# The start of a hybrid decoder step: normalization in written order, query weights loaded by contraction tiles, and products without a reader between them

## The chip, the cores and the metric

The program runs on one core of a Trainium2 chip. The time of a run is the device time of that core in microseconds (us). Three runs of the kernel before gave 1644.03, 1644.74 and 1642.79 us; their median, 1644.03 us, is the number that the predicted time is compared with. The engines are named as in the profile: PE (matrix products), ACT, DVE and POOL (elementwise work, casts, copies), SP (it issues transfers). POOL and ACT issue transfers as well. Every engine takes its instructions in the order in which they stand in its own queue, and waits at the head of that queue until what the instruction needs is there.

## The reference

One layer of a decoder is applied to 512 prompt rows with 16 learned rows ahead of them, and to 8 x 4 sample rows with caches: T = 560 rows of width 2048 in all. What matters here is its beginning:

```python
def rmsnorm(x, g):
    xf = x.astype(jnp.float32)
    y = xf * lax.rsqrt(jnp.mean(xf * xf, axis=-1, keepdims=True) + RMS_EPS)
    return (y * g.astype(jnp.float32)).astype(x.dtype)
...
    h = rmsnorm(x, g_pre)
    q, k, v, ga, cb, cc, ch, gc, ma, mc = jnp.split(h @ w_in, split_offsets(), axis=-1)
...
    a = attend(q, k, v, b_sb).reshape(bsz, t, D_ATTN) * jax.nn.silu(ga)
    u = cc * ch
    u_ext = jnp.concatenate([conv_hist.astype(u.dtype), u], axis=1)
    c = cb * causal_conv(u_ext, w_conv, b_conv) * jax.nn.silu(gc)
    merged = (jax.nn.sigmoid(ma + b_gate[:D_MODEL]) * (a @ w_pa)
              + jax.nn.sigmoid(mc + b_gate[D_MODEL:]) * (c @ w_pc))
    y = x + rmsnorm(merged @ w_out, g_post)
```

Everything is float32. There are 8 heads of width 128, so a head's queries are 128 columns of w_in. The sample rows read keys and values from pages that page_table names.

## The kernel before, in words

A float32 product is made of three products of reduced-precision parts: every operand is split into a high part (a cast, on ACT) and a low part (operand minus high part, on DVE), and high x high, high x low and low x high are summed. A product of 2048 input columns is a sum over 16 contraction tiles k of 128 columns; one group of 48 matmuls (16 k, three parts) gives 128 output columns for some 280 rows.

**The start stage** (all code up to `stx.close()`) normalizes the input and computes the queries of the first four heads (`FIRST = 4`), of which the later stages make use. Its parts:

- The rows come in five tiles (`XT`): x0 and x1 hold prompt rows 0 to 255, x2 and x3 the next 248, x4 the last 8 prompt rows, the sample rows and half of the learned rows (48 rows); x2 holds the other learned rows. They are loaded by SP into three buffers `xt`.
- `norm_stats(i)` loads a tile, squares and sums each row on ACT (`sq`), and takes Ln and Exp for a first reciprocal root (`rtmp`); `newton` sharpens it in five small operations on DVE (`rs`).
- The gain `g_pre` is spread over the partitions by 32 small matmuls on PE into four PSUM tiles `g_ps`, copied to `g_bc` by `g_copy(c)`. Ten 128x512 products of a constant, with no reader (`warm_up`, tile `tp`), stand ahead of them.
- `norm_half(c, x)` multiplies half a tile by `rs` and `g_bc` on DVE (`hn`), transposes it on PE in two groups of four (into the PSUM tiles z, of which there are three, and tp), casts each group to `h_hi` on ACT and subtracts on DVE into `h_lo`. One half covers eight contraction tiles k.
- `q_load(h)` loads the weights of head h in two units of eight contraction tiles (`raw`, 512 KB), and casts them (`whi`, ACT). The low parts (`wlo`) come later, by `low()`, on DVE.
- `START` cuts the rows into the 256 of x0 and x1 and the other 296. For the first 256, the products with the high weights of all four heads run before the tiles x4, x2, x3 are normalized, and the products with the low weights (`parts (2,)`) after it, together with the 296 rows.

What sets the order: PE's, ACT's, DVE's, POOL's and SP's instructions are ordered at build time by a scheduler with a model of time. `tc.keep_in_program_order` (`pin`) holds an instruction to the written order; `tc.high_priority` moves one ahead. Before the change, the multiplications, low parts and newton steps on DVE are pinned, the transposes and the casts of h on ACT have high priority, and the query products, the casts of weights and the loads are free.

**Buffers**: `wraw` has five tiles `raw`, `whl` three each of `hi` and `lo` (they serve the whole kernel), and `sp` is a pool of the start stage alone; what other pools place over its memory has to wait for `stx.close()`, that is for its last reader.

**After the start stage**: the tables `bsb` (the heads' bias), `pt_i` (the page table, from which POOL reads 32 register values by `value_load` before it can issue page loads), `bg_n`, `wc_n` and `st_n` are loaded by POOL. Then `head_now(0)` computes k, v and another query projection on PE (line 252 before), while `q_proj` stores the queries of the first heads through `qn` into `q_scr` by POOL; the decode steps read them back as `qb` (POOL), multiply them with pages `kpage` on DVE (`pr`) and sum on ACT or DVE. `natural` transposes k and v on PE into tp, copies them to `nat` and `ks`, and POOL stores them (`out<-nat`); `nat` is one buffer, so that v's copy waits until k's store has landed.

Of the kernel before, what the change touches and what calls it, by code (L numbers as in the profile page):

```python
# [60 lines left out]
def hybrid_step_kernel(  # L61
# [58 lines left out]
    def load_x(xt, i):  # L120
        r = 0
        for n, src, r0 in XT[i][0]:
            nc.sync.dma_start(xt[r:r + n, :], {"p": xp, "m": meta_tokens, "s": xs}[src][r0:r0 + n, :])
            r += n

    def rstd_of(eng, out, ss, tmp, n, w=1, later=False):

        v, r, t = (tmp[:n, i * w:(i + 1) * w] for i in range(3))
        act.activation(r, ss, AF.Ln, bias=eps_c[:n], scale=1.0 / D)
        act.activation(r, r, AF.Exp, scale=-0.5)  # L130
# [39 lines left out]
    for c, mk in enumerate((mm_ps, mm_ps, mm_ps, z_ps)):  # L170
# [11 lines left out]

    start_ps = cycle((z_ps, z_ps, z_ps, t_ps))

    def norm_stats(i):

        n = sum(r[0] for r in XT[i][0])
        xt = sp.tile([P, D], F32, name="xt", bufs=3)[:n]
        load_x(xt, i)
        ss = sp.tile([P, 1], F32, name="ss", bufs=5)[:n]  # L190
# [3 lines left out]
        with tc.high_priority():  # L194
            act.activation(sq, xt, AF.Square, accum_out=ss)
            newton = rstd_of(dve, rs, ss, tmp, n, later=True)
        return (i, n, xt, rs), newton

    def norm_half(c, x):
# [7 lines left out]
        low = []  # L207
        for kq in range(2):
            pt = next(start_ps)()
            pv = pt[:, :4 * n].rearrange("p (k t) -> p k t", t=n)  # L210
            with tc.high_priority(2000):
                for k in range(4):
                    pe.transpose(out=pv[:, k, :], in_=hn[:, (4 * kq + k) * P:(4 * kq + k + 1) * P],
                                 identity=ident[:n, :n])
            k0 = 8 * c + 4 * kq
            for r0, r1, t0 in XT[i][1]:
                dst = (slice(None), slice(k0, k0 + 4), slice(t0, t0 + r1 - r0))
                with tc.high_priority(2000):
                    act.copy(h_hi[dst], pv[:, :, r0:r1])
                low.append((h_lo[dst], pv[:, :, r0:r1], h_hi.bitcast(F32)[dst]))  # L220

        def lows():
            for x in low:
                pin(dve.tensor_sub(*x))
# [1097 lines left out]
```

## Time and profile before

| | |
|---|---|
| median of three runs | 1644.03 us |
| the profiled execution | 1641.85 us |
| its span, first to last instruction | 1640.3 us |
| PE busy in the span | 1594.9 us (97%) |
| DVE, ACT, POOL busy | 1251.8, 970.1, 232.4 us |
| mean granted PE clock | 0.99 |
| first product after the start stage (line 252) | at 86.40 us |

The profiled execution stands 1.55 us above its own span and 2.18 us under the median of the runs. A row of the timeline gives the start in us from the first instruction, the length in us, the engine, the line, the operation, the tiles written and read, their shapes and a count where equal instructions follow each other; a bracket gives the idle time before it and what ended it. Rows of the windows give, for a stretch of time, the busy time of each engine with its count of instructions, then the granted PE clock, the share of the DMA engines and GB/s. Matmuls overlap each other, so the pace of a row of matmuls is read from start to start, not from their lengths.

### The profile page before, as it was taken

What the parts mean: (1) busy time and instruction counts of PE and PEld (TensorE: products, weight loads), DVE (VectorE), ACT (ScalarE), POOL (GpSimd) and SP (SyncE); (2) the same over time, 40 slices, a digit from 0 to 9 for tenths busy, and PEclk for the clock granted to TensorE, in tenths of its full rate; (3) what the DMA queues carried; (4) which work ended last, traced back from release to release, by engine and by line L of the source; (5) the groups of instructions that cost most, each with busy time, mean ns of one, the idle gap of its engine ahead of it and who ended that gap; (6) DMA issues with size and microseconds to landing.
All of it is one profiled execution on the core that took longest, in us unless ns stands there. A gap on an engine that the chain in (4) does not pass through costs nothing.

```text
span 1640.3 us, 31584 instructions
## 1 busy us (share of the span) xinstructions
PE 1594.9 (97%) x12176; PEld 1531.3 (93%) x12176; DVE 1251.8 (76%) x1707; ACT 970.1 (59%) x2529; POOL 232.4 (14%) x414
## 2 busy tenths in 40 slices
PE   7999999999999999999999999999999999999996
PEld 6999999999999999999999999989867699999995
DVE  4537887797988988888988888876555567877774
ACT  5237887745765655655677667685544543455552
POOL 0033233322101010101011010013122110000000
PEclk7999999999999999999999999999999999999998
DMA  9255454445544444443455454446887555433336
GB/s 228 70 179 152 155 160 139 146 128 170 157 147 136 136 135 122 127 142 111 137 164 161 149 174 148 135 125 204 283 261 222 172 152 179 154 106 94 104 87 216
DMA packets 306492, 252.72 MB, mean 154 GB/s; under 512 B 11457, under 2 KB 276741, under 8 KB 305237
## 3 DMA queue, kind: packets, MB, share of 16 engines
q1 hardware_dynamic: 277605, 159.73, 34.1%
q0 software_dynamic: 28016, 88.80, 16.5%
q8 instruction: 95, 1.56, 0.4%
q10 hardware_dynamic: 720, 2.17, 0.4%
q14 instruction: 56, 0.46, 0.1%
HBM read 217.95 MB, written 32.71 MB: 153 GB/s over the span
## 4 chain that ended last, share of the span: by engine, by line
PE 75%; ACT 6%; DMA 5%; DVE 5%; issue 3%; POOL 0%; DVEq 0%; SPq 0%; POOLq 0%; ACTq 0%
PE mm L887 24%; PE mm L252 24%; PE o L887 19%; ACT junk L695 3%; PE tp L784 2%; ACT whi L236 2%; DMA raw<-in_w_in 2%; PE z L614 1%; PE o L624 1%; DVE pr L689 1%; DVE wlo L237 1%; DMA gt<-gate_scr 1%; PE z L545 1%; PE z L887 1%; DMA kpage<-in_cache_k 1%
## 5 line engine op out<-in xcount | busy, mean ns | idle before, releaser
L236 ACT CAST whi<-raw 128x1024 fp32r<-128x1024 f32 x251 | 263.1, 1050 | 258.5 <-PE o L887 79.3
L237 DVE TENSOR_TENSOR wlo<-raw,whi 128x1024 fp32r<-128x1024 f32 x251 | 306.4, 1221 | 58.0 <-ACT whi L236 46.1
L887 PE MATMUL mm<-h_hi,whi 128*128 128x272 f32 (+1 forms) x1152 | 333.5, 290 | 2.8 <-ACT whi L236 2.8
L887 PE MATMUL mm<-h_lo,whi 128*128 128x272 f32 (+1 forms) x1152 | 332.1, 288 | 0.0
L887 PE MATMUL mm<-h_hi,wlo 128*128 128x272 f32 (+1 forms) x1152 | 331.3, 290 | 0.0
L887 PE MATMUL o<-t_hi,whi 128*128 128x272 f32 (+1 forms) x864 | 252.2, 292 | 8.5 <-ACT o L901 5.9
L887 PE MATMUL o<-t_hi,wlo 128*128 128x272 f32 (+1 forms) x864 | 249.9, 289 | 1.4 <-DVE wlo L237 1.4
L887 PE MATMUL o<-t_lo,whi 128*128 128x272 f32 (+1 forms) x864 | 249.6, 289 | 0.0
L237 DVE TENSOR_TENSOR wlo<-s,whi 128x1024 fp32r<-128x1024 f32 x126 | 154.2, 1224 | 101.5 <-ACT whi L236 101.2
L887 PEld LDWEIGHTS mm<-h_hi,whi 128*128 128x128 f32 x1152 | 217.3, 189 | 5.5 <-ACT whi L236 3.7
L887 PEld LDWEIGHTS mm<-h_hi,wlo 128*128 128x128 f32 x1152 | 216.3, 189 | 0.6 <-DVE dr L412 0.4
L887 PEld LDWEIGHTS mm<-h_lo,whi 128*128 128x128 f32 x1152 | 216.8, 188 | 0.1
L695 ACT ACTIVATE junk<-pr 128x128 f32<-128x128 f32 x592 | 182.7, 309 | 28.3 <-DVE pr L689 16.1
L236 ACT CAST whi<-s 128x1024 fp32r<-128x1024 f32 x126 | 131.6, 1044 | 97.5 <-PE o L887 31.0
L252 PE MATMUL mm<-h_hi,whi 128*128 128x280 f32 (+1 forms) x640 | 187.1, 293 | 0.0
L252 PE MATMUL mm<-h_hi,wlo 128*128 128x280 f32 (+1 forms) x640 | 187.0, 293 | 0.0
L252 PE MATMUL mm<-h_lo,whi 128*128 128x280 f32 (+1 forms) x640 | 186.7, 292 | 0.0
L887 PEld LDWEIGHTS o<-t_hi,whi 128*128 128x128 f32 x864 | 162.7, 188 | 15.1 <-ACT o L901 7.0
L887 PEld LDWEIGHTS o<-t_hi,wlo 128*128 128x128 f32 x864 | 162.9, 189 | 2.3 <-DVE wlo L237 2.2
L887 PEld LDWEIGHTS o<-t_lo,whi 128*128 128x128 f32 x864 | 163.4, 189 | 0.0
L689 DVE TENSOR_TENSOR pr<-kpage,qb 128x1024 f32<-128x1024 f32 x128 | 152.3, 1218 | 8.4 <-DMA kpage<-in_cache_k 4.0
L252 PEld LDWEIGHTS mm<-h_hi,whi 128*128 128x128 f32 x640 | 120.5, 188 | 0.7
(389 smaller groups left out, 3398.2 us busy)
## 6 DMA issues: line engine op xcount, KB each, us to landing
raw<-in_w_in SPq DMA_DIRECT2D x192, 512.0 KB, 4.3
kpage<-in_cache_k POOLq DMA_DIRECT2D x64, 256.0 KB, 3.4
qb<-q_scr POOLq DMA_DIRECT2D x32, 512.0 KB, 5.3
vpage<-in_cache_v POOLq DMA_DIRECT2D x64, 256.0 KB, 5.7
raw<-in_w_out SPq DMA_DIRECT2D x32, 512.0 KB, 4.0
gate_scr<-g POOLq DMA_DIRECT2D x32, 272.0 KB, 3.2
gt<-gate_scr POOLq DMA_DIRECT2D x16, 544.0 KB, 4.2
raw<-in_w_pc SPq DMA_DIRECT2D x16, 512.0 KB, 5.8
```

Source lines behind the costliest of these rows:

```text
L236: act.copy(hi, x)
L237: dve.tensor_sub(lo, x, hi.bitcast(F32))
L252: pe.matmul(o, lhsT=w, rhs=r[:, t0:t1], start=(k == 0 and n == 0), stop=(k == nk - 1 and n == 2))
L545: pe.matmul(zt[:m, c0:c0 + n], lhsT=l[:, s0:s0 + m], rhs=r[:, ts:ts + n], start=(c0 == 0 and i == 0), stop=(i == 2), skip_group_check=True)
L614: pe.matmul(o, lhsT=l, rhs=x, start=False, stop=(i == len(ops) - 1), skip_group_check=True)
L624: pe.matmul(ot[:, ts - NMETA:ts - NMETA + n], lhsT=l[:m, st, :], rhs=x[:m, c0:c0 + n], start=False, stop=(g == GROUPS[-1] and i == 2), ski ...
L689: dve.tensor_mul(pr, kt.unsqueeze(1).broadcast_to([P, 2, 512]), qt))
L695: act.activation(junk, pr[:, t, h * P:(h + 1) * P], AF.Copy, accum_out=z_all[:, pg, b, 4 * hf + h, 2 * i + t:2 * i + t + 1])
L784: pe.matmul(po[32 * j:32 * (j + 1), :], lhsT=lhs, rhs=rhs, start=(pg == 0), stop=(pg == NPG), tile_position=(0, 32 * j), skip_group_check= ...
L887: pe.matmul(o, lhsT=l[:, k, :], rhs=r, start=(start and k == 0 and m == 0), stop=(stop and k == 7 and m == 2), skip_group_check=True)
```

## The change

The start stage is written anew; nothing after `stx.close()` is touched.

- The weights are no longer loaded by head but by contraction tiles: each of eight loads (`q_load`) fetches two contraction tiles for all four heads (runs of 512 columns in place of 128; 512 KB as before). `q_high` and `q_low` split one load, and `q_chunk(c)` runs all 24 products (four heads, two k, three parts) of it for the first 256 rows. The accumulators of the four heads share two PSUM tiles mm.
- The whole stage (loads, squares, Ln, Exp, transposes, casts, products) is pinned to the written order, which now interleaves the eight chunks with the normalization of x2, x4 and x3.
- The tile x2 is loaded right behind the first three loads of weights, x4 when a buffer is free, x3 behind all weights. `newton` of x2 and x4 runs on POOL.
- `g_copy(2)` and `g_copy(3)` run on ACT.
- 18 further 128x512 products without a reader: four after g's second and fourth group (`warm_up(4)`), four and six between the transposes of x0 and x1 (`keep_warm`). The transposes also use the PSUM tile o.
- Two weight parts of five tiles each (40 KB a partition) now lie in the pool `sp` in place of five high parts and three raw tiles (32 KB).

```diff
-            with tc.high_priority(2000):
-                for k in range(4):
-                    pe.transpose(out=pv[:, k, :], in_=hn[:, (4 * kq + k) * P:(4 * kq + k + 1) * P],
-                                 identity=ident[:n, :n])
+            for k in range(4):
+                pin(pe.transpose(out=pv[:, k, :], in_=hn[:, (4 * kq + k) * P:(4 * kq + k + 1) * P],
+                                 identity=ident[:n, :n]))
...
+    def q_load():
+        c = len(q_raw)
+        raw = wraw.tile([P, 8, P], F32, tag="raw", name="raw")
+        pin(nc.sync.dma_start(raw.rearrange("p (k h) c -> p k (h c)", k=2),
+                              win[2 * c * P:2 * (c + 1) * P, GATE_Q:GATE_Q + FIRST * P].rearrange(
+                                  "(k p) c -> p k c", p=P)))
+        q_raw.append(raw)
+
+    def q_part_tile(c, name):
+        if c < 3:
+            return whl.tile([P, 8, P], F32R, tag=name, name="w" + name)
+        return sp.tile([P, 8, P], F32R, name="w" + name, bufs=NC - 3)
...
+    def q_chunk(c):
+        for h in range(FIRST):
+            for k in (2 * c, 2 * c + 1):
+                q_product(q_o[h], h, k, 0, k == 0 and h % 2 == 0, k == KD - 1)
+
+    def keep_warm(n):
+        pt = o_ps()
         for _ in range(n):
+            pin(pe.matmul(pt, lhsT=neg_one, rhs=neg_one.unsqueeze(1).broadcast_to([P, 4, P]), start=True, stop=True))
+
+    X = [None] * 5
+    X[0], X[1] = x_load(0), x_load(1)
+    for _ in range(3):
+        q_load()
+    X[2] = x_load(2)
+    X[0], newton0 = norm_stats(X[0])
     g_copy(0), g_copy(1)
+    g_copy(2), g_copy(3)
+    X[1], newton1 = norm_stats(X[1])
     newton0(pin)
+    h00, l00 = norm_half(0, X[0])
+    keep_warm(4)
+    h01, l01 = norm_half(1, X[0])
+    keep_warm(6)
+    h00()
     newton1(pin)
+    q_high()
+    h10, l10 = norm_half(0, X[1])
+    h01()
     l00()
+    h11, l11 = norm_half(1, X[1])
+    h10()
+    X[4] = x_load(4)
+    for _ in range(2):
+        q_load()
...
+    l10()
+    q_high()
+    q_low()
+    h11()
+    q_chunk(0)
     l01()
+    q_low()
     l11()
+    q_high()
+    q_chunk(1)
+    X[2], newton2 = norm_stats(X[2], pool)
+    q_low()
+    for _ in range(2):
+        q_load()
+    q_chunk(2)
+    X[4], newton4 = norm_stats(X[4], pool)
+    newton2()
+    h20, l20 = norm_half(0, X[2])
...
+    q_chunk(4)
+    h40, l40 = norm_half(0, X[4])
+    l21()
+    q_high()
+    h40()
+    q_low()
+    h41, l41 = norm_half(1, X[4])
+    q_chunk(5)
...
+    q_chunk(6)
+    q_high()
+    q_low()
+    X[3], newton3 = norm_stats(X[3])
+    q_chunk(7)
+    newton3(pin)
+    h30, l30 = norm_half(0, X[3])
+    h30()
+    h31, l31 = norm_half(1, X[3])
...
+    for h in range(FIRST):
         q_o[h] = (z_ps if h < 3 else mm_ps)()[:, :START[1][1] - START[1][0]]
+        for k in range(KD):
+            q_product(q_o[h], h, k, 1, k == 0, k == KD - 1)
     stx.close()
```

**First place: PE and ACT from the start to the first query product.** On PE before, the end of the transposes (line 213) of x0, those of x1's first half ("z x8") and the first query products (297):

```order
L213 MATMUL z<-ident,hn 128x128
L213 MATMUL tp<-ident,hn 128x128
L213 MATMUL z<-ident,hn 128x128 x8
L297 MATMUL mm<-h_hi,whi 128x256 x3
L213 MATMUL z<-ident,hn 128x128
L213 MATMUL tp<-ident,hn 128x128
```

On PE in the changed kernel, from the gain's last products (line 176) on; the lines 158 and 338 are products without a reader, 218 the transposes, 323 the query products, and "z x12" are the second group of x1's first half and both groups of its second half:

```order
L176 MATMUL z<-g_hl,pick 128x128 x8
L158 MATMUL tp<-neg_one 128x512 x4
L218 MATMUL z<-ident,hn 128x128 x8
L338 MATMUL o<-neg_one 128x512 x4
L218 MATMUL z<-ident,hn 128x128 x4
L218 MATMUL tp<-ident,hn 128x128 x4
L338 MATMUL o<-neg_one 128x512 x6
L218 MATMUL o<-ident,hn 128x128 x4
L218 MATMUL z<-ident,hn 128x128 x12
L323 MATMUL mm<-h_hi,whi 128x256
L323 MATMUL mm<-h_lo,whi 128x256
L323 MATMUL mm<-h_hi,wlo 128x256
```

All 32 transposes of x0 and x1 now stand ahead of the first query product, where before three query products stood ahead of the last eight. On ACT before, behind the first tile's squares:

```order
L195 ACTIVATE sq,ss<-xt 128x2048
L309 CAST whi<-raw 128x1024
L129 ACTIVATE rtmp<-ss,eps_c 128x1
L309 CAST whi<-raw 128x1024
L130 ACTIVATE rtmp<-rtmp 128x1
L195 ACTIVATE sq,ss<-xt 48x2048
L219 CAST h_hi<-z 128x4x128 x2
```

And on ACT in the changed kernel:

```order
L185 COPY g_bc<-mm 128x512
L185 COPY g_bc<-z 128x512
L202 ACTIVATE sq,ss<-xt 128x2048
L130 ACTIVATE rtmp<-ss,eps_c 128x1
L131 ACTIVATE rtmp<-rtmp 128x1
L226 CAST h_hi<-z 128x4x128 x2
L312 CAST whi<-raw 128x1024
L226 CAST h_hi<-z 128x4x128
```

The Exp of x1 no longer stands behind two casts of weights; two copies of the gain stand ahead of x1's squares.

**Second place: DVE ahead of the first chunk.** Before, from the first multiplication of x1 (line 205) to the last low part of x1 (224):

```order
L205 SCALAR_TENSOR_TENSOR hn<-xt,rs,g_bc 128x1024
L224 TENSOR_TENSOR h_lo<-z,h_hi 128x4x128 x3
L224 TENSOR_TENSOR h_lo<-tp,h_hi 128x4x128
L205 SCALAR_TENSOR_TENSOR hn<-xt,rs,g_bc 128x1024
L224 TENSOR_TENSOR h_lo<-z,h_hi 128x4x128 x3
```

In the changed kernel, from the first multiplication of x1 (line 211) on; 230 are the low parts of h, 317 those of the weights:

```order
L211 SCALAR_TENSOR_TENSOR hn<-xt,rs,g_bc 128x1024
L230 TENSOR_TENSOR h_lo<-z,h_hi 128x4x128 x2
L211 SCALAR_TENSOR_TENSOR hn<-xt,rs,g_bc 128x1024
L230 TENSOR_TENSOR h_lo<-o,h_hi 128x4x128
L230 TENSOR_TENSOR h_lo<-z,h_hi 128x4x128
L317 TENSOR_TENSOR wlo<-raw,whi 128x1024
L230 TENSOR_TENSOR h_lo<-z,h_hi 128x4x128
L230 TENSOR_TENSOR h_lo<-tp,h_hi 128x4x128
L317 TENSOR_TENSOR wlo<-raw,whi 128x1024
```

The sixth row is new at this place; the seventh reads the z tile into which the last of x1's transposes is to be written.

**Third place: POOL around the end of the start stage.** Before, from the last of the 32 register loads (line 666; the first two tables, bsb and pt_i, stand at the very start of the queue) to the first page load (line 667); two stores of the queries and the first store of `qn` follow behind the third page load:

```order
L666 TENSOR_LOAD pt_i
L666 ISA x2
L359 DMA qt_scr<-qf 128x256 x4
L377 DMA bg_n<-in_b_gate 32x128
L379 DMA wc_n<-in_w_conv 24x128
L380 DMA wc_n<-in_b_conv 8x128
L382 DMA st_n<-in_state_conv 16x1024
L667 ISA
L667 DMA kpage<-in_cache_k 128x512
```

In the changed kernel, from the same stores of `qf` on (734 are the register loads, 735 the page loads):

```order
L426 DMA qt_scr<-qf 128x256 x4
L441 DMA bsb<-in_b_sb 128x8
L442 DMA pt_i<-in_page_table 1x16x2
L445 DMA bg_n<-in_b_gate 32x128
L447 DMA wc_n<-in_w_conv 24x128
L448 DMA wc_n<-in_b_conv 8x128
L450 DMA st_n<-in_state_conv 16x1024
L540 DMA qt_scr<-qr 128x288 x2
L734 TENSOR_LOAD pt_i
L734 ISA x2
L735 ISA
L735 DMA kpage<-in_cache_k 128x512
```

The loads of bsb and pt_i, and with them all 32 register loads, moved from the start of the queue to behind the start stage: 17 of them stand ahead of the first store of `qn`, one between that store and the next row, four ahead of the second store, four ahead of the third and six ahead of the fourth.

More of the change, by code (lines that the diff above doesn't have):

```diff
@@ L193, in norm_stats @@
         tmp = sp.tile([P, 4], F32, name="rtmp", bufs=5)
[L194 to L197, printed above, removed]
+        pin(act.activation(sq, xt, AF.Square, accum_out=ss))
+        return (i, n, xt, rs), rstd_of(eng, rs, ss, tmp, n, later=True, fix=pin)
     def norm_half(c, x):
@@ L206, in norm_half @@
                                      op0=ALU.mult, op1=ALU.mult))
-        low = []
+        parts = []
         for kq in range(2):
@@ L282, in hybrid_step_kernel @@
     START = ((HM, HM + 256), (HM + 256, T))
-    w_low = []
-    def low(n=1):
-        for _ in range(n):
-            unit, raw = w_low.pop(0)
-            lo = whl.tile([P, 8, P], F32R, tag="lo", name="wlo")
-            pin(dve.tensor_sub(lo, raw, unit[0].bitcast(F32)))
-            unit.append(lo)
-    def q_part(o, ws, n, parts, start, stop):
-        t0, t1 = START[n]
-        for k in range(KD):
-            for m in parts:
-                pe.matmul(o, lhsT=ws[k // 8][m // 2][:, k % 8, :], rhs=(h_lo if m == 1 else h_hi)[:, k, t0:t1], start=(start and k + m == 0),
-                          stop=(stop and k == KD - 1 and m == parts[-1]), skip_group_check=True)
@@ L300, in hybrid_step_kernel @@
-    q_w, q_o = [], []
-    def q_load(h):
-        q_w.append([])
-        for src in win_srcs(GATE_Q + h * P):
-            n = len(w_low)
-            raw = w_load(src, sp if n >= 5 else wraw)
-            hi = sp.tile([P, 8, P], F32R, name="whi", bufs=2 * FIRST - 3) if n >= 3 else \
-                whl.tile([P, 8, P], F32R, tag="hi", name="whi")
-            act.copy(hi, raw)
-            q_w[h].append([hi])
-            w_low.append((q_w[h][-1], raw))
-    x0, newton0 = norm_stats(0)
-    x1, newton1 = norm_stats(1)
@@ new lines, in q_part_tile, with q_high, q_low, q_product @@
+    def q_part_tile(c, name):
+        if c < 3:
+            return whl.tile([P, 8, P], F32R, tag=name, name="w" + name)
+        return sp.tile([P, 8, P], F32R, name="w" + name, bufs=NC - 3)
+    def q_high():
+        c = len(q_hi)
+        q_hi.append(q_part_tile(c, "hi"))
+        pin(act.copy(q_hi[c], q_raw[c]))
+    def q_low():
+        c = len(q_lo)
+        q_lo.append(q_part_tile(c, "lo"))
+        pin(dve.tensor_sub(q_lo[c], q_raw[c], q_hi[c].bitcast(F32)))
+    def q_product(o, h, k, n, start, stop):
+        t0, t1 = START[n]
+        hi, lo = (by_k(x[k // 2])[:, k % 2, h, :] for x in (q_hi, q_lo))
+        for m, (l, r) in enumerate(((hi, h_hi), (hi, h_lo), (lo, h_hi))):
+            pin(pe.matmul(o, lhsT=l, rhs=r[:, k, t0:t1], start=(start and m == 0), stop=(stop and m == 2),
+                          skip_group_check=True))
@@ L326, in hybrid_step_kernel @@
+    X[4] = x_load(4)
+    for _ in range(2):
+        q_load()
+    for i in range(2):
+        o = mm_ps()
+        q_o += [o[:, 0:256], o[:, 256:512]]
+    l10()
[3 more added lines that the diff above has]
+    q_chunk(0)
     l01()
[L327 to L328 removed]
+    q_low()
     l11()
[L330 to L336 removed]
```

101 lines of the change are left out of this document (48 added, 53 removed).

## The prediction

> **What bounds the kernel now.** I read the page first: its span, the busy shares, and the row of the PE clock by fortieths of the span.
>
> ```profile
> span 1640.3 us, 31584 instructions
> PE 1594.9 (97%) x12176; PEld 1531.3 (93%) x12176; DVE 1251.8 (76%) x1707; ACT 970.1 (59%) x2529; POOL 232.4 (14%) x414
> PEclk7999999999999999999999999999999999999998
> ```
>
> PE is busy for 97% and has a full clock nearly everywhere: a change elsewhere is worth only what it takes from PE's 45.4 us without work. The first fortieth has a clock of 7, so the windows of the start come next.
>
> ```profile
> 0.00:10.00 10.00, 8.62 (x42) 7.05 (x42) 4.00 (x17) 3.78 (x5) 2.15 (x9) 0.96 0.80 231
> 10.00:26.30 16.30, 5.84 (x24) 4.70 (x24) 8.56 (x15) 11.76 (x19) 0.00 (x0) 0.50 1.16 253
> 26.30:29.70 3.40, 3.31 (x15) 3.32 (x16) 1.63 (x3) 2.41 (x4) 0.00 (x0) 0.50 0.99 230
> 29.70:86.50 56.80, 54.07 (x428) 53.10 (x427) 29.16 (x50) 17.03 (x34) 2.21 (x4) 1.00 0.36 97
> ```
>
> From 10 to 26.3 us PE works 5.84 of 16.3 us, at half clock (0.50). It is dense from 26.3, and the clock is full from 29.7; the stage then runs to 86.4 with 2.7 us lost. So PE starts late. The timeline says on whom it waits, and gives its paces.
>
> ```profile
> 1.34 4.62 PE L157 MATMUL tp<-neg_one 128*128 128x512 f32 x10 [1.34 <-DVE neg_one L112]
> 10.81 1.94 PE L213 MATMUL z<-ident,hn 128*128 128x128 f32 x8 [0.85 <-DVE hn L205]
> 22.07 1.97 PE L213 MATMUL z<-ident,hn 128*128 128x128 f32 x8 [6.80 <-DVE h_lo L224]
> 26.39 1.01 PE L297 MATMUL mm<-h_hi,whi 128*128 128x256 f32 x3 [2.35 <-ACT h_hi L219]
> 44.93 1.06 PE L213 MATMUL z<-ident,hn 128*128 128x128 f32 x8 [2.48 <-DVE hn L205]
> 61.32 2.06 PE L297 MATMUL mm<-h_hi,wlo 128*128 128x256 f32 x16
> 63.21 0.30 PE L297 MATMUL z<-h_hi,wlo 128*128 128x296 f32 x1
> 71.41 0.30 PE L297 MATMUL z<-h_hi,whi 128*128 128x296 f32 x1
> 77.95 0.52 PE L297 MATMUL o<-h_hi,wlo 128*128 128x256 f32 x3
> 86.40 0.29 PE L252 MATMUL mm<-h_hi,whi 128*128 128x280 f32 x1
> ```
>
> The first query product stands at 26.39, the stage ends at 86.40. Paces at full clock: 16 products of 256 rows take 63.21 - 61.32 = 1.89 us, 0.119 each; 48 of 296 rows take 77.95 - 71.41 = 6.54 us, 0.136 each; a transpose (44.93: 1.06 less the last one's 0.27, over 7) 0.11. At half clock a transpose takes 0.22 (10.81) and a constant product of 512 about 0.43 (1.34).
>
> **The change, step by step.** Its queries need what they needed: 192 x 0.119 = 22.9 and 192 x 0.136 = 26.2 us. What moves is when they begin. ACT and DVE carry the chain up to there.
>
> ```profile
> 6.01 1.91 ACT L195 ACTIVATE sq<-xt 128x2048 f32<-128x2048 f32 x1 [3.79 <-DMA xt<-in_x_prompt]
> 8.37 0.20 ACT L130 ACTIVATE rtmp<-rtmp 128x1 f32<-128x1 f32 x1
> 10.28 1.91 ACT L195 ACTIVATE sq<-xt 128x2048 f32<-128x2048 f32 x1 [1.71 <-DMA xt<-in_x_prompt]
> 20.73 1.04 ACT L219 CAST h_hi<-z 128x512 fp32r<-128x512 f32 x2
> 26.70 2.01 ACT L309 CAST whi<-raw 128x1024 fp32r<-128x1024 f32 x2
> 36.68 1.92 ACT L195 ACTIVATE sq<-xt 128x2048 f32<-128x2048 f32 x1 [4.49 <-DMA xt<-in_x_prompt]
> 39.16 1.90 ACT L195 ACTIVATE sq<-xt 128x2048 f32<-128x2048 f32 x1
> 8.54 0.14 DVE L133 TENSOR_SCALAR rtmp<-ss 128x1 f32<-128x1 f32 x1
> 9.38 1.28 DVE L205 SCALAR_TENSOR_TENSOR hn<-xt,rs,g_bc 128x1024 f32<-128x1024 f32 x1
> 26.65 1.28 DVE L224 TENSOR_TENSOR h_lo<-z,h_hi 128x512 fp32r<-128x512 f32 x2
> 56.23 2.35 DVE L290 TENSOR_TENSOR wlo<-raw,whi 128x1024 fp32r<-128x1024 f32 x2
> ```
>
> So a tile's squares, Ln and Exp cost ACT 39.16 - 36.68 = 2.48, newton costs DVE 0.84, half a tile `hn` 1.28 (1.2 in a row), a cast of h 0.5, of weights 1.0, a low part of h 0.65, of weights 1.2.
>
> x0 is as before: Exp done at 8.57, first half of `hn` at 10.7. On ACT the copies of g 2 and 3 come next. Their products stand behind four new constant products on PE; with the clock halved from 9.2 they end near 9.8 and 11.1, the second copy at 11.9. Thus x1's squares, ready at 10.28, run from 11.8 to 14.3: 1.5 us lost, but the Exp no longer waits behind casts of weights. newton and `hn` of x1 end at 16.7. The 18 constant products take 18 x 0.43 = 7.7 us at half clock, partly in place of waiting: the last six end near 18.4, x1's transposes start then. ACT casts them to 20.1; DVE does h_lo (to 21.0), wlo 0 (22.1) and the low part (22.7) that frees the third z tile for the last transposes. The first chunk starts at **23.4**, 3.0 us earlier than 26.39, and, unlike before, with nothing left over: the low products of x0 and x1 are in it.
>
> From there the sum for PE is 22.9 + 26.2, transposes of x2 and x3 16 x 0.11 twice = 3.5, of x4 (48 rows) 1.0, and waits. I followed ACT and DVE through the eight chunks by these prices: one chunk takes PE 2.86 us, DVE in the same time has one wlo, one `hn` and two low parts (3.7 us) for the chunks 3 to 5, with a lead of two chunks that it uses up. One wait is left, for x4's second half (0.9), and 0.3 before the 296 rows. The 3.0 us of waiting ahead of 22.8 probably drops the clock again, as at 9.2; dense work brought it back within 3.4 us (26.3 to 29.7), so the first chunk loses 1.6. Stage end: 23.4 + 22.9 + 26.2 + 4.5 + 1.2 + 1.6, less 0.3 that overlaps = **79.5**, 6.9 us earlier: 3.0 from the start, the rest from what lay between 26.39 and 86.40 (half clock to 29.7 with eight transposes of x1 in it, 2.7 us of waiting).
>
> *Loads.* Up to x2 they are 3 x 1.05 + 3 x 0.52 = 4.7 MB: 2.3 by 10 us at 231 GB/s, the rest at 253 by 19.5; its squares come at 25. On SP, x4's first piece waits until `hn` of x0 frees a buffer (13.2), and the weights 3 to 7 and x3 stand behind it; the first of them, weights 3, is cast at 30. Runs of 2 KB in place of 512 bytes aren't shown: bounds are no gain and the rate of the row at 26.30; I take none, since the slack hides it. *newton on POOL* isn't shown either: five operations between the fill of 128x1 and the select of 128x128 are 0.5 to 1.6 us; at either end PE's wait is 0.9 or up to 1.4.
>
> ```profile
> 0.47 0.10 POOL L1310 MEMSET const-float32-1.0<- 128x1 f32 x1
> 2.77 0.31 POOL masks.py:199 TENSOR_SCALAR_AFFINE_SELECT ident<-ident 128x128 f32<-128x128 f32 x1
> L666 POOLq TENSOR_LOAD <-pt_i x32: 282/289/502, 9.6 to 28.3; - x32
> 87.02 0.51 POOL L377 DMA_DIRECT2D bg_n<-in_b_gate  x1 [5.69 <-PE mm L297]
> 89.05 1.67 POOL L667 DMA_DIRECT2D kpage<-in_cache_k  x3
> 111.41 2.18 POOL L681 DMA_DIRECT2D qb<-q_scr  x3 [1.78 <-issue]
> 115.78 1.23 DVE L689 TENSOR_TENSOR pr<-kpage,qb 128x1024 f32<-128x1024 f32 x1 [3.15 <-DMA qb<-q_scr]
> 118.16 0.38 PE L442 MATMUL tp<-ident,raw 128*128 128x128 f32 x2
> 117.48 5.70 DMA out<-nat
> 123.92 0.28 PE L445 MATMUL tp<-ident,raw 128*16 128x128 f32 x1 [1.13 <-ACT nat L443]
> ```
>
> *What is given back.* The larger pool of the stage now lies over bsb and pt_i, so the register loads follow the stage's end E on POOL. They were hidden (9.6 to 28.3 us, 0.60 apart). Now: six table loads of 0.51 from E+0.6 to 3.7; two stores 1.1; three register and page loads 3.5; 14 more register loads 8.4; the four stores of `qn` with 15 register loads and two query stores between end at E+28.8; `qb` starts 1.8 later at E+30.6 (before: 111.41, E+25.0), and `pr` 4.4 behind it at E+35.0. DVE's copies `nat` and `ks` stand behind `pr`; PE's transposes into tp wait for them until E+36.7. They were due at E+31.8 (118.16), now behind 27 more products (3.5 us), at E+35.3. The store of `nat` follows `pr` by 1.7 and lands 5.7 later, v's copy 0.7 behind: PE at E+43.1, due at 36.4 + 3.5 = 39.9. It waits 3.2 in all, 1.13 before: **2.1 us lost**. Bounds: nothing, if the loads of registers run two to one faster than here, and 6.7 more if each took the longest row's 502 ns in place of 289.
>
> The weights of k are no new wait: the three shared high tiles come free with the last head's k 1, 3 and 5, 5.7 to 4.1 us before E, a cast and a subtraction take 2.2. The order behind that is the scheduler's own, and differs on DVE and ACT in single rows; I allow 2 us to either side. Sum: 6.9 - 2.1 = 4.8 us, from 1641.85 (span 1640.3 and 1.55 around it) to 1637.05; the median stood 2.18 above that execution, so **1639.2 us**.
>
> **The clock, and a rule.** 24 transposes between 10 and 26.3 left the clock at 0.50, while 15 instructions in 26.30 to 29.70, eight of them transposes, brought it to 1.00. In the stretch 12.6 to 16.1 of the new order stand as many transposes and four constant products; I take it that the clock rises there. The Trainium skill, "TensorE: Matmul & The Clock Gate", section "Part 4: PE-mode transpose", says that a transpose doesn't count as PE-busy the same way; the first window agrees, the second neither way. By that rule the clock would stay low here, which is the second rival. The same page, section "Why this matters for your kernels", holds that one window of idle PE (some 3 us) puts the clock back, which speaks for the loss of 1.6 that I took; without it the stage would end at 77.9.
>
> **The rivals.**
> 1. *Nothing is given back and the clock holds*: the register loads find slack and PE's wait before chunk 0 is short. 77.9 for the stage, 8.5 us, 1635.5. For it: 0.60 us apart is twice the load's 289 ns. Against: POOL takes its queue in order.
> 2. *The clock stays low until the products run*: constant products and transposes at double price put chunk 0 at 26.3 and the full clock at 29.7, as before. By the same steps E = 82.6, 3.8 - 2.1 = 1.7 us, 1642.3.
> 3. *The loads set the pace*: x2, asked for at 26 us, came 10 us later (36.68, a wait of 4.49 for it). From 28 us on its arrival delays PE one for one; at 31 E is 83.9 and the time 1643.6. Against: it is asked for at 6 us now.
> 4. *Slower, by POOL*: all 32 register loads stand ahead of `qb`, and beyond the 2.1 us every extra 0.1 us of each costs PE 3.2. From 0.85 us a load the kernel is over 0.2% slower; at 0.9 it loses 9.6 more, 1648.8. For it: nothing but PE is behind that queue. Against: they were 0.60 apart with DMA engines full.
>
> **How the numbers follow.** Forecast 0.48, rivals 0.14, 0.13, 0.13, 0.12. About 0.2%, 3.3 us, is what a measurement here can tell from no change; the forecast lies 4.8 off, and 0.04 of its chance falls inside. Faster: 0.44 + 0.14 = 0.58; same: 0.04 + 0.26 = 0.30; slower 0.12. The range takes in the first three rivals and their allowances, 1634.5 to 1645.5, and leaves the fourth and a little below out.
>
> **What would show it.** The first query product near 23.4, with x1's last transposes waiting for h_lo by 3 us; a clock of 1.0 between 16 and 22.9 and a dip behind it; the first product of k near 79.5; register loads between E+5 and E+29; `qb` at E+30.6; waits of 3.2 us at k's and v's transposes. A stage end past 83, or a PE wait behind E above 6 us, would make it wrong.

## The result, and the profile after

| | before | after |
|---|---|---|
| median of 20 runs each, taken together | 1643.89 us (1641.24 to 1647.73) | 1648.55 us (1641.97 to 1654.06) |
| the profiled execution | 1641.85 us | 1647.67 us |
| its span | 1640.3 us | 1646.1 us |
| first product of the first query chunk | 26.39 us | 22.21 us |
| end of the start stage (first product of k) | 86.40 us | 77.63 us |

The changed kernel is slower: ratio 1.0033, interval 1.0023 to 1.0042. The page of its profile, with the same three rows as before:

```profile
span 1646.1 us, 31611 instructions
PE 1601.0 (97%) x12194; PEld 1536.4 (93%) x12194; DVE 1247.2 (76%) x1695; ACT 970.2 (59%) x2531; POOL 236.8 (14%) x424
PEclk9999999999999999999999999999999999999998
```

PE is busy 6.1 us longer and stands still for 45.1 us, against 45.4. Nothing in these rows says where the time went, and the first fortieth, the one that the change is about, now has a full clock. So I went by place. The windows of the start stage (columns as in the table of before: PE, PEld, DVE, ACT, POOL busy with counts, granted clock, DMA share, GB/s) and three rows of PE's timeline:

```profile
10.00:20.00 10.00, 9.94 (x50) 8.50 (x50) 6.38 (x11) 6.71 (x12) 0.00 (x0) 0.72 0.99 220
20.00:30.00 10.00, 8.64 (x72) 8.20 (x71) 8.44 (x11) 9.62 (x15) 3.19 (x7) 1.00 0.84 228
30.00:77.60 47.60, 46.84 (x373) 46.39 (x372) 22.99 (x35) 15.89 (x31) 4.79 (x8) 1.00 0.34 108
```
```profile
21.80 0.66 PE L218 MATMUL z<-ident,hn 128*128 128x128 f32 x4 [1.12 <-DVE h_lo L230]
22.21 0.36 PE L323 MATMUL mm<-h_hi,whi 128*128 128x256 f32 x1
77.63 0.29 PE L258 MATMUL mm<-h_hi,whi 128*128 128x280 f32 x1
```

The start stage does more than was forecast: it ends 8.8 us earlier, with a full clock from the first query product on. The loss is behind it. To see where, I compare when PE begins the matmul that has as many matmuls left to run as in before (the programs differ by the 18 constant products at the start alone). The lead of the changed kernel is 8.8 us at 86.4, 4.2 at 187.9, 4.3 at 358.0, 1.6 at 383.5, and at 411.2 it is 5.2 us **behind**, which stays to the end (5.7). Two places took it, on the clock of before: 4.8 us go between 108 and 136 us, and 9.5 between 380 and 411. Wherever leads are compared below, the times are those of before.

The first is the one that the prediction named: the register loads behind the stage. The row of these loads, then rows of the timelines of POOL, DVE and PE in order of time:

```profile
L734 POOLq TENSOR_LOAD <-pt_i x32: 283/288/549, 83.1 to 106.9; - x32
```
```profile
78.39 0.54 POOL L441 DMA_DIRECT2D bsb<-in_b_sb  x1 [24.84 <-DMA raw<-in_w_in]
108.05 0.50 POOL L546 DMA_DIRECT2D q_scr<-qn  x1 [3.56 <-ACT raw L586]
110.44 2.18 POOL L749 DMA_DIRECT2D qb<-q_scr  x3 [1.90 <-issue]
115.70 1.23 DVE L757 TENSOR_TENSOR pr<-kpage,qb 128x1024 f32<-128x1024 f32 x1 [6.92 <-DMA qb<-q_scr]
117.05 0.27 DVE L516 COPY ks<-tp 32x128 f32<-32x128 f32 x1
117.37 0.66 PE L510 MATMUL tp<-ident,raw 128*128 128x128 f32 x4 [3.20 <-DVE ks L516]
```

The loads run to 106.9, the last store of `qn` comes behind them, `qb` behind that, `pr` waits for `qb` with `ks` behind it on DVE, and PE waits 3.2 us for `ks`. The products behind that wait run 0.23 us apart instead of 0.13: the clock is at half from 118.0 to 121.4.

The second place, which no part of the prediction named, is the chain of waits at the passage from the heads to the gates (start, us, what). Its one wait of 7.1 us on PE is also more than the 6 us behind the stage that the prediction gave as a sign of being wrong.

```profile
386.21 1.23 DVE s L983
387.44 0.02 SPq L236
...
387.49 12.85 DMA raw<-in_w_in
...
401.61 1.22 DVE wlo L243
402.82 1.13 DVE raw L978
403.96 0.36 DVE c L981
...
404.36 4.93 PE o L955 x24
```

A weight tile takes 12.85 us to land; DVE, and behind it PE, wait for it. The DMAs issued between 386 and 391 us in the changed kernel (KB each, median us from issue to landing), and then the tiles' row of before, whose other issues there are four stores of 8 and 16 KB:

```profile
qb<-q_scr POOLq DMA_DIRECT2D x3, 512.0 KB, 6.6
raw<-in_w_in SPq DMA_DIRECT2D x2, 512.0 KB, 13.1
kpage<-in_cache_k POOLq DMA_DIRECT2D x3, 256.0 KB, 9.9
```
```profile
raw<-in_w_in SPq DMA_DIRECT2D x2, 512.0 KB, 4.1
```

In before the same two tiles were issued at 388.72 and 389.82 and the six transfers of the second decode part (`qb` and `kpage`, 2.25 MB; "the burst" from here) only from 394.47 on. Now the burst goes out from 386.26, 1.2 us **ahead** of the tiles (387.49, 388.59). PE then has nothing to do for 7 us and comes out of that at half clock, as the windows show:

```profile
390.00:397.30 7.30, 7.27 (x58) 7.05 (x57) 0.50 (x1) 3.78 (x4) 0.08 (x1) 1.00 0.91 286
397.30:404.40 7.10, 0.04 (x1) 0.04 (x1) 3.94 (x5) 0.06 (x1) 0.00 (x0) 0.78 0.37 109
404.40:409.30 4.90, 4.90 (x26) 4.90 (x27) 4.90 (x7) 3.79 (x15) 0.57 (x1) 0.62 0.33 96
```

The scheduler has turned two things round there. ACT's rows at the end of the heads, in before (a bracket names the semaphores that a row waits for):

```
CAST h_hi<-r_5020 128x2x274 [waits PE_49] x4
CAST whi<-s 128x1024 [waits DVE_49,Activation_49]
COPY raw<-mm 128x272 [waits PE_49]
COPY raw<-mm 128x8
ACTIVATE o<-mm 128x272 [waits PE_49]
COPY nat<-tp 128x512 [waits DMASW6_49,DMASW5_49,PE_49]
CAST whi<-s 128x1024 [waits DVE_49]
```

and in the changed kernel:

```
CAST t_hi_5035<-x 128x548 [waits DVE_49]
COPY raw<-mm 128x272 [waits PE_49]
COPY raw<-mm 128x8
ACTIVATE o<-mm 128x272 [waits PE_49]
COPY nat<-tp 128x512 [waits DMASW5_49,DMASW6_49,PE_49,Activation_49]
CAST whi<-s 128x1024 [waits DVE_49,Activation_49]
CAST whi<-s 128x1024 [waits DVE_49]
```

The last heads' `nat` stands ahead of the first `whi<-s`. So the last store of the heads is issued 6.6 us earlier (382.73 against 389.29); the burst goes out 1.6 to 2.0 us behind its landing in both profiles. The first cast of `s`, whose use frees the buffers of the two tiles, comes no earlier (379.25 against 379.18).

### The profile page after: what moved, and what is told of

Read it like the earlier page. It is cut to its first block, busy times and chain, and to the rows that moved or that the text cites. A ratio compares the mean times of both kernels' runs of the same rounds, so it can differ in the third digit from the quotient of the medians.

```text
span 1646.1 us, 31611 instructions
## 1 busy us (share of the span) xinstructions
PE 1601.0 (97%) x12194; PEld 1536.4 (93%) x12194; DVE 1247.2 (76%) x1695; ACT 970.2 (59%) x2531; POOL 236.8 (14%) x424
## 4 chain that ended last, share of the span: by engine, by line
PE 75%; ACT 6%; DVE 5%; DMA 4%; issue 3%; DVEq 0%; POOL 0%; POOLq 0%; ACTq 0%; SPq 0%
PE mm L955 24%; PE mm L258 24%; PE o L955 19%; ACT junk L763 2%; DMA raw<-in_w_in 2%; PE tp L852 2%; ACT whi L242 2%; PE z L682 1%; DVE pr L757 1%; PE o L692 1%; DVE wlo L243 1%; DMA gt<-gate_scr 1%; PE z L613 1%; PE z L955 1%; PE z L1239 0%
## 5 line engine op out<-in xcount | busy, mean ns | idle before, releaser
L242 ACT CAST whi<-raw 128x1024 fp32r<-128x1024 f32 x251 | 262.6, 1049 | 270.1 <-PE o L955 77.6
L955 PE MATMUL o<-t_hi,whi 128*128 128x272 f32 (+1 forms) x864 | 253.0, 293 | 14.0 <-DVE c L981 10.3
L955 PEld LDWEIGHTS mm<-h_hi,whi 128*128 128x128 f32 x1152 | 217.4, 189 | 7.0 <-ACT whi L242 5.2
L955 PEld LDWEIGHTS mm<-h_lo,whi 128*128 128x128 f32 x1152 | 216.8, 188 | 0.1
L955 PEld LDWEIGHTS o<-t_hi,whi 128*128 128x128 f32 x864 | 163.5, 189 | 20.8 <-DVE c L981 11.8
L258 PEld LDWEIGHTS mm<-h_lo,whi 128*128 128x128 f32 x640 | 121.1, 189 | 0.6
```

The lines of the kernel that those rows point to most:

```text
L242: act.copy(hi, x)
L258: pe.matmul(o, lhsT=w, rhs=r[:, t0:t1], start=(k == 0 and n == 0), stop=(k == nk - 1 and n == 2))
L955: pe.matmul(o, lhsT=l[:, k, :], rhs=r, start=(start and k == 0 and m == 0), stop=(stop and k == 7 and m == 2), skip_group_check=True)
```

## The experiments

All ratios are to runs of before on the same chip: 6 to 12 runs of each kernel beside 12 to 35 of before. "E" is the end of the start stage in the profile of the run, "lead" how far PE is ahead of before's profile at 358.0 and at 411.2 us of it, counted as above. E and the leads are of one profiled execution, the ratio is of all runs; the two differ most in e4, whose profiled execution took 1665.4 us at a median of 1656.2.

The theories that the first expectations name for the second place: A, the burst takes the DMA engines from the two tiles that DVE and PE wait for; B, ACT's order does it by itself, with nat ahead of the conversions of s. The register loads are the cause argued for the first place.

| run | E | lead at E | at 358 | at 411 | ratio (95%) |
|---|---|---|---|---|---|
| the changed kernel | 77.63 | 8.8 | 4.3 | -5.2 | 1.0033 (1.0023 to 1.0042) |
| e1 gate | 81.39 | 5.0 | -0.3 | -0.8 | 1.0006 (0.9996 to 1.0017) |
| e2 before, gate | 85.00 | 1.4 | 0.8 | 3.4 | 0.9996 (0.9986 to 1.0006) |
| e3 loads early | 75.01 | 11.4 | 7.9 | -1.1 | 1.0010 (0.9998 to 1.0022) |
| e4 before, loads late | 85.91 | 0.5 | -9.8 | -21.6 | 1.0087 (1.0074 to 1.0101) |
| e5 gate, loads early | 78.05 | 8.4 | 8.5 | 6.7 | 0.9983 (0.9972 to 0.9994) |
| e6 loads early, decode later | 78.02 | 8.4 | 7.9 | 6.7 | 0.9970 (0.9955 to 0.9985) |
| e7 decode later | 75.04 | 11.4 | 5.7 | 4.5 | 0.9991 (0.9979 to 1.0004) |
| e8 changed again | 78.06 | 8.3 | 3.7 | -3.1 | 1.0035 (1.0024 to 1.0047) |
| e9 before, decode later | 83.95 | 2.5 | 2.4 | 0.7 | 1.0001 (0.9991 to 1.0010) |
| e10 as e6, no constants | 75.37 | 11.0 | 8.8 | 7.9 | 0.9951 (0.9936 to 0.9966) |
| e11 as e6, again | 81.53 | 4.9 | 5.1 | 4.1 | 0.9973 (0.9961 to 0.9986) |
| e12 changed, no constants | 78.02 | 8.4 | 3.6 | -5.8 | 1.0035 (1.0021 to 1.0048) |

### e1 and e2: hold the burst until the tiles have landed

```
...
-            dec_step(1 if 4 < n <= 20 else 1 + n % 2, "logits")
+            dec_step(0 if n == 1 else 3 if n == 2 else 1 if 4 < n <= 20 else 1 + n % 2, "logits")
...
+                        if said == "logits" and (hf, b) == part[0]:
+                            pool.tensor_copy(qt[0:1, 0, 0:1], held[6][0:1, 0, 0:1])
...
+                        if said == "logits" and (hf, b) == part[0] and pg < 3:
+                            pool.tensor_copy(kt[0:1, 0:1], held[6][0:1, 0, 0:1])
...
+    held = []
...
-        return [w_load(src[k, m]) for k, m in ((k1, c1), (k1, c2), (k2, c2), (k2, c1))]
+        ws = [w_load(src[k, m]) for k, m in ((k1, c1), (k1, c2), (k2, c2), (k2, c1))]
+        held.extend(ws)
+        return ws
```

POOL writes one element of each buffer of the burst from the seventh of these weight tiles, so the burst can't be issued before that tile has landed; and the decode steps of the first group of products (up to two) are put off to the second group.

> The changed kernel with one edge more: behind the heads, the first three qb and the first three kpage transfers of the second decode part (2.25 MB, issued at 386.3 to 389.4 us in the profile of the changed kernel) wait until the third weight tile of the second pair has landed, by one-element copies on POOL; to have that tile at hand, the first decode step of that part is taken one group later. Theory A (collision: the two weight tiles issued at 387.49 and 388.59 took 12.8 and 13.4 us instead of 4 because the burst was on the queues, so TensorE waited 7.1 us at 397.3 and ran at half clock for 6.8 us behind it): the two tiles land in 4 to 5 us, the wait at 397 is under 2 us, and the whole takes 1636 to 1640 us, below before. Theory B (the wait comes from the order of the rows on ACT and DVE at 378 to 383, where whi<-s stands behind nat): the tiles may land early, but the time stays within 2 us of 1648.5.

> The kernel before with the same edge and the same later step. Control for the first run: in its profile the burst starts at 394.5, when the same two tiles have landed already (issued 388.72 and 389.82, 4.1 us). Theory A: within 3 us of 1643.9, since what the edge waits for is there. If it gains as much as the changed kernel does, the edge or the later step is worth something of its own and the first run tells nothing about the change.

The two tiles of e1 (issued 392.08 and 393.17) and PE's longest waits between 80 and 412 us (total, times, longest):

```profile
raw<-in_w_in SPq DMA_DIRECT2D x2, 512.0 KB, 4.5
```
```profile
PE tp L510 <- DVE ks L516: 3.3, 1, 3.3
PE tp L543 <- ACT qn L545: 1.5, 1, 1.5
PE mm L959 <- DVE wlo L243: 0.7, 1, 0.7
```

The tiles land in 4.5 us, and the wait near 400 is gone, although ACT's rows are in the changed order here too: between 390 and 411 us the lead of e1 grows by 2.6 us, where that of the changed kernel falls by 6.4. So theory A holds for the collision. Theory B keeps a part of its own: between 380 and 390 us e1 loses 3.0 us, as much as the changed kernel, with three waits of 0.6 to 0.7 us on ACT and DVE that before does not have; e2, with the gate and the order of before, loses nothing there. The whole gains 0.27%, and its median of 1643.98 us misses A's 1636 to 1640; those 3.0 us are a part of what is missing. The decode steps that were put off are nearly even: in e2 they gain 2.5 us up to 411 and take 3.0 by 488. The control does not change.

### e3 and e4: the register loads early, and late in the kernel before

```
+    bsb = const.tile([P, H], F32, name="bsb")
+    pt_i = const.tile([1, DB * NPG], I32, name="pt_i")
+    pool.dma_start(bsb, b_sb.broadcast_to([P, H]))
+    pool.dma_start(pt_i, page_table.rearrange("b p -> (b p)").unsqueeze(0))
     stx = ExitStack()
```

e4 has the same two tiles in the kernel before, its two DMAs where they were, and ahead of `stx.close()`:

```
+    dve.tensor_copy(bsb[0:1, 0:1], qf[0:1, 0:1])
+    dve.tensor_copy(pt_i.bitcast(F32)[0:1, 0:1], qf[0:1, 0:1])
```

> The changed kernel with bsb and pt_i in the pool of constants, so that their DMAs and the 32 register loads stand at the start of POOL's queue again. Theory of the prediction (the loads behind the stage hold up the q_scr stores and so qb and pr): no register load behind 78 us, the wait of 3.2 us at 117 and the half clock behind it gone, the first pr at about 108 instead of 115.7, and between 80 and 200 us 4 to 5 us less than in the changed kernel. For the whole: if nothing else happens 1643.5 to 1645; if the collision at 388 depends on when the heads end, anything between 1633 and 1650. Rival (the qb chain is set by the q_scr stores' own latencies, not by the loads): first pr stays at 113 to 116 and the time within 1.5 us of the changed kernel.

> The kernel before with bsb and pt_i in the pool of constants but written once by DVE from the last query block, so that their DMAs and the 32 register loads come behind the start stage, as in the changed kernel; the start stage itself is untouched. Theory of the prediction: 2 to 6 us slower than before at 200 us, and if that goes to the end 1646 to 1650. Rival (the loads are covered): within 1 us of 1643.9.

The loads and the longest waits of PE in e3, then in e4:

```profile
L734 POOLq TENSOR_LOAD <-pt_i x32: 282/289/500, 9.6 to 31.6; - x32
```
```profile
PE o L955 <- DVE c L981: 6.5, 1, 6.5
PE tp L510 <- ACT junk L763: 2.7, 1, 2.7
```
```profile
L668 POOLq TENSOR_LOAD <-pt_i x32: 283/289/757, 84.1 to 111.8; - x32
```
```profile
PE o L889 <- DVE c L915: 8.7, 1, 8.7
PE tp L444 <- ACT junk L697: 7.0, 1, 7.0
```

e3 gains 0.23%, and its first `pr` comes at 108.4, as expected; but a wait of 2.7 us and 3.4 us of half clock are left at the same transposes, and the wait near 400 is there. From E to 200 us e3 loses 3.4 us, the changed kernel 4.6: the 4 to 5 us less that were expected there did not come. e4 is the run that tells most. Its start stage is that of before, and yet its profiled execution loses 10.3 us by 200 (2 to 6 were expected, and a median of 1646 to 1650 where 1656.2 came) and, between 358 and 411, 11.8 us more around the wait for `c` (8.7 of waiting, and a lower clock around it): a kernel without any of the change's start has the second loss too. In e4, as in every run with nat ahead of whi<-s and no gate, the burst (400.44) goes out ahead of the two tiles (401.56, 402.66). So an early end of the stage isn't needed for them to meet; what all runs in which they meet share is the order of the rows. No run turned these rows alone, so that the order is the cause rests on this agreement. It came with the register loads late in e4, and stayed with them early in e3; what in the scheduler's model chooses it was not settled.

### e5, e6 and e7: both losses taken away

e5 is e1 and e3 together. e6 has the early loads of e3 and, in place of the gate, this; e7 has this alone:

```
         khi, klo = k_split(np_, k_proj(h))
-        dec_step(1, "part")
+        dec_step(1 if h else 0, "part")
         vhi, vlo = v_proj(h, np_)
-        dec_step(1, "part")
+        dec_step(1 if h else 0, "part")
         q_proj(NOW + h)
-        dec_step(2, "part")
+        dec_step(2 if h else 4, "part")
```

> The changed kernel with the edits of the first and the third run together: the burst waits for the third weight tile of the second pair, and bsb and pt_i are loaded at the start. If the collision at 388 and the register loads are two separate losses, their gains add: 0.27% and 0.23% of the changed kernel, so about 0.5%, a ratio to before of 0.997 to 0.9995 (1638 to 1642 us where before takes 1642.4). If they are one loss seen twice, the ratio stays at 1.000 to 1.001.

> The changed kernel with bsb and pt_i loaded at the start, and with the first four decode steps of head 0 taken together behind its last projection instead of one by one; no edge on the burst. Behind the heads the order of ACT's rows is again that of before: whi<-s ahead of o<-mm and nat. Theory A' (the collision needs the order with nat ahead of whi<-s, because the last stores of the heads and with them the burst come forward while the weight loads do not): the wait at 397 is gone without any edge on the burst, the wait at 110 to 117 is gone as well (nat and ks no longer stand behind pr on DVE), ratio to before 0.995 to 0.998. Rival (the burst collides whenever the start stage ends early, whatever the order): 6 to 9 us of wait at 390 to 405 remain and the ratio is 0.999 to 1.002.

> The changed kernel with that shift of the first four decode steps alone; the register loads still come behind the start stage. Theory A' : no wait at 397, as in the sixth run. For the register loads: if they cost by way of pr standing ahead of nat and ks on DVE, they cost nothing here and the ratio is that of the sixth run within 0.1%; if they cost by the q_scr stores themselves (ACT waits for them with qn), 0.1 to 0.3% more than the sixth run.

In e6 and e7 ACT has whi<-s ahead of nat again. e6's DMAs issued between 381 and 388 us, and the longest waits of PE in e6 and in e7 between 80 and 412:

```profile
qb<-q_scr POOLq DMA_DIRECT2D x3, 512.0 KB, 7.6
raw<-in_w_in SPq DMA_DIRECT2D x2, 512.0 KB, 5.7
kpage<-in_cache_k POOLq DMA_DIRECT2D x3, 256.0 KB, 8.2
```
```profile
PE tp L513 <- ACT nat L511: 2.3, 2, 1.8
PE o L955 <- DVE wlo L247: 0.9, 1, 0.9
```
```profile
PE tp L513 <- ACT nat L511: 3.9, 2, 3.5
PE tp L543 <- ACT qn L545: 1.2, 1, 1.2
PE o L955 <- DVE wlo L243: 0.9, 1, 0.9
```

The tiles are issued at 382.41 and 383.51, the burst at 384.18: less than 2 us in the other direction, and they land in 5.7 us, with 0.9 us of waiting left. Between 380 and 390 us e6 loses 1.6 us. The wait at 110 to 117 was expected to be gone; 1.8 us of it are left, for `nat` (1.1 in before). The gains of e1 and e3 add (0.27% and 0.23% against 0.50% in e5). e6 beats both kernels, 0.9970. e7 shows that the register loads still cost where `pr` no longer stands ahead of nat: 0.21% more than e6 (the intervals just overlap). The way is POOL's queue: PE waits 1.2 us for `qn`, whose buffer waits for the stores into `q_scr`, and k's store of `nat` is issued 35.2 us behind E where e6 has 27.6, so that PE waits 3.5 us for v's copy instead of 1.8.

### e8 and e9: the changed kernel again, and a control

> The changed kernel once more, on the chip of these runs, for its ratio and a second profile. Its start stage ended at 77.6, 81.4 and 75.0 us in three profiles of the same rows, with three histories of the clock in the first 20 us; a fourth should lie between 75 and 82. Theory A: the wait of 6 to 8 us at 395 to 405 in this profile too. Ratio 1.002 to 1.0045.

> Control for the sixth and seventh run: the kernel before with the first four decode steps of head 0 taken together behind its last projection, nothing else. Its rows behind the heads have whi<-s ahead of nat already, and its wait there is 1.1 us at 124. Theory A' (the shift only takes away what the change had brought): ratio to before 0.998 to 1.001. Rival (the shift is a gain of its own, and the start stage's lead is not what the sixth run shows): 0.994 to 0.997, as in the sixth run.

The longest waits in e8:

```profile
PE o L955 <- DVE c L981: 3.4, 1, 3.4
PE tp L510 <- DVE ks L516: 2.8, 1, 2.8
```

The wait near 400 is 3.4 us, not 6 to 8, so this part of the expectation missed; with the half clock around it, it still takes 6.7 us between 358 and 411. e9's shift does nothing for the kernel before (1.0001), so what e6 and e7 gain from it is what the change had brought in.

### e10, e11 and e12: without the products that nobody reads

Both calls of `keep_warm` and the `warm_up(4)` behind g's products are left out, 18 constant products; in e10 from e6's kernel, in e12 from the changed one. e11 is e6 again, beside e10.

> The kernel of the sixth run without the 18 products that nobody reads (four behind the second and the fourth of g's products, four and six among x0's transposes). Theory of the prediction (they keep the clock up between g's products and the queries; without them TensorE stands still for 1 to 3 us there and the clock is at half when the first chunk comes, as in before from 9.2 to 29.7): first chunk product at 21 to 23 us but at half clock for one or two steps of 3.4 us, stage end 79.5 to 82 instead of 75 to 78, ratio 1.5 to 4 us above the sixth run. Rival (transposes and g's products keep it as well without them): stage end 75 to 78 and the ratio of the sixth run within 0.1%.

> The kernel of the sixth run once more, on the chip of these runs, as the yardstick of the tenth and for its ratio: 0.995 to 0.9985, no wait over 1 us between 380 and 410.

> The changed kernel without the 18 products that nobody reads, nothing else (register loads late, no edge on the burst; behind the heads nat still stands ahead of whi<-s on ACT). Theory from the tenth run (the fillers stand in TensorE's queue between g's products and x0's and x1's transposes, and where the clock is granted late they take 0.43 us each and hold up the first chunk by up to 4 us): the gain of the tenth run over the eleventh, 0.1 to 0.3%, comes here too, ratio 1.0005 to 1.0025; stage end at 75 to 77; the wait near 400 stays. Rival (their price depends on the rest): ratio 1.003 to 1.0045, as the changed kernel has it.

In PE's timeline of e10, x0's transposes; then the windows of e10 from 11.35 to 21.6, and the one from 10 to 20 of e11:

```profile
11.13 2.79 PE L220 MATMUL z<-ident,hn 128*128 128x128 f32 x12 [1.11 <-DVE hn L213]
13.71 1.06 PE L220 MATMUL tp<-ident,hn 128*128 128x128 f32 x4
```
```profile
11.35:14.76 3.41, 3.41 (x16) 3.02 (x15) 2.47 (x7) 3.35 (x7) 0.00 (x0) 0.50 1.16 338
14.76:18.17 3.41, 1.72 (x13) 1.26 (x12) 3.41 (x6) 3.29 (x6) 0.00 (x0) 1.00 0.97 200
18.17:21.60 3.43, 2.98 (x15) 2.77 (x14) 3.43 (x6) 2.12 (x3) 0.00 (x0) 0.50 1.01 179
```
```profile
10.00:20.00 10.00, 10.00 (x36) 8.25 (x36) 5.19 (x14) 5.12 (x9) 0.00 (x0) 1.00 0.96 271
```

The forecast for e10 missed its sign. Without the constants the clock does fall once more (18.17 to 21.6), but the first chunk starts at 19.60 and the stage ends at 75.4. In e11's execution the clock came late, with a recorded rise at 20.7 (its window shows 1.00 because nothing had been recorded by then; the constant products in it are 0.43 us apart, the pace of half clock), PE was full to 20 us with them, and the first chunk started at 26.14. e10's median is 3.2 us under e11's, with intervals that just overlap. e12, whose profile has the wait near 400 (5.1 us), ends its stage at 78.02 (75 to 77 was expected) and is no faster than e8, as its rival had it. So whether the constants pay is open. The single executions say this much: where the clock rises late, the stage ends at 78.0 without them (e12, a rise at 17.0) and at 81.4 and 81.5 with them (e1, e11); where it first rises at 4.5 to 4.7, it ends at 75.4 without them (e10) and at 75.0 with them (e3, e7). The runs do not give one price.

## Why the prediction was wrong, step by step

- **The start stage** was right in its mechanism and small in size. First chunk 22.21 instead of 23.4, because x1's last transposes waited 1.12 us for h_lo and not 3.0; the clock did not dip, and the 1.6 us set aside for that were not lost. Stage end 77.63 (78.06 in e8) instead of 79.5, since the rest of the stage took 0.9 us more than the sum: a gain of 8.8 (8.3) instead of 6.9. The dip had been argued from the fall at 9.2 us in before, as one that waiting brings, and that reading was wrong: in the 3.41 us ahead of that fall PE was busy all the time, with the gain's products. That waiting can bring a dip, e10 shows (1.72 of 3.41 us busy, then half clock). What the step did not have is how much this depends on when the clock rises: with the same rows of PE up to there, E was 75.0 where it rose at 4.6 to 4.7 us and stayed (e3, e7), 77.6 to 78.1 where it rose at 5.3 to 6.4 and fell again 3.4 us later, 81.4 and 81.5 where it rose at 20.4 and 20.7 (e1, e11). The four profiles with the start stage of before ended at 84.0 to 86.4. The changed kernel's runs spread over 12.1 us, those of before over 6.5.
- **What is given back** was right in its mechanism and too small. Loads from E+5.5 to E+29.3 (forecast E+5 to E+29), `qb` at E+32.8 (30.6), `pr` at E+38.1 (35.0), waits of 1.1 us for `qn` and 3.2 us at k's transposes on PE (the forecast 3.2 was the sum of k's and v's, and v's did not wait), and 3.4 us at half clock behind the second, which the sum did not have. From E to 358 us the loss is 4.5 us. e8 and e5, with stages that end alike (78.06 and 78.05) and the loads late and early, lose 4.7 and gain 0.1: 4.8 us for 2.1, inside the bounds. The loads are not all of it, though: with them early, the loss from E to 358 is at most 0.5 us for stage ends of 78.0 and later (e5, e6, e11), but 2.2 and 3.5 us for 75.4 and 75.0 (e10, e3). What an end as early as that gives back by another wait, no run took away.
- **"The order behind that is the scheduler's own"**, with 2 us allowed to either side, is the step that failed. It cost 9.5 us in the profiled execution and 6.7 in e8, between 358 and 411 us: 3.0 (4.1) at 380 to 390 with the turned rows, gate or no gate, and the rest by the collision. e6, e7, e10 and e11, with the rows as in before, lose 0.9 to 1.3 in that stretch; e1 and e5, gated, 0.5 and 1.8, and 3.3 and 4.4 by 488, where their put-off steps have been made up. The sum with the measured sizes: 8.8 - 4.5 - 9.5 = -5.2 us, what stands at 411. The step asked which rows differ, not what they start: two transfers on different queues, whose order hangs on less than 2 us.
- **The rivals.** The slower one gave 1648.8, near the median, and that is luck: it wanted register loads 0.85 us apart and more, and they were 0.59 apart where nothing stood between them, as before. "The clock stays low until the products run" came half true in two of the eight profiles of the changed start with the constant products: the first chunk at 25.98 and 26.14 (forecast 26.3) and stage ends of 81.4 and 81.5 (forecast 82.6), but with the full clock 5 us ahead of the products and not behind them. The loads set no pace: ACT began x2's squares at 23.93 without a wait for the tile.
- **The clock at 12.6 to 16.1** rose at 15.6, as argued. The rule that stood against it (the Trainium skill, "TensorE: Matmul & The Clock Gate", section "Part 4: PE-mode transpose": transposes don't count as PE-busy the same way) does not hold for these float32 transposes, as e10 shows: 16 of them at 0.21 us and nothing else filled 11.35 to 14.76, and the clock was 1.00 from there. The window of before that seemed to agree with it, 10 to 26.3, had PE idle for 10.5 of its 16.3 us, and could not decide.

## What to carry to other kernels

A gain in one stage moves everything that its end sets free: list the transfers that will start earlier, with their sizes, and ask which transfer that somebody waits for will now stand behind them. Where a change alters the order in a later stage, compare the order of issues on the DMA queues as well as the rows of the engines. An edge that holds a burst back until the needed tile has landed is a cheap test of such a meeting; once that is shown, moving the step that issues the burst (here the first decode steps) may cost less than the edge.

## What the hardware showed that I had not expected

- Two tiles of 512 KB on SP's queue took 12.9 and 13.4 us with 2.25 MB of POOL's transfers issued around them, and about 4 us without. The Trainium skill, "DMA: Bandwidth & Descriptors", section "Queues, rings and completion order", says that a DMA engine takes packets from the queues with work in turn. The trace agrees in part: from 391 to 398 us packets of both ran side by side (411 of POOL's queue with 1.39 MB, 1347 of SP's with 0.68 MB), but from 388 to 391 it was 215 of POOL's (0.81 MB) and 2 of SP's, though the first tile had been issued at 387.49. Why the tiles' packets began so late is open.
- The clock of the first 20 us differs from execution to execution under the same rows of PE: it rose for the first time at 4.6 to 6.4 us in six profiles and at 20.4 and 20.7 in two; e6 and e11, 6.2 and 20.7, are one program. Where it fell again, it fell and rose in steps of 3.41 us. A step with PE busy 1.72 of 3.41 us was followed by half clock, one with 2.98 by full clock (e10). But a busy PE is not enough: in before, the clock fell at 9.23 behind a step with PE busy 3.41 of 3.41 us, and in e11 the four steps ahead of the one that raised it had PE busy all through at half clock. What sorts these steps is how much of them g's products took, which use 16 partitions. Counting steps from the recorded rises over the first 24 us, in all 14 profiles a step at half clock with PE full raised the clock where they took at most 0.72 us of it, and not where they took 0.86 or more; a step at full clock with PE full held it up to 1.93 us of them and lost it from 1.97 on. So the differing starts look like a matter of where the steps fall among these products. That they count for less was not tested by itself.
